# Up-projection of a conv-gated MLP: the Strassen weight sums move from VectorE to accumulating DMAs, and one plain feature tile becomes a Strassen one

## The chip, the core and the metric

The kernel runs on one core of a Trainium2 chip. The metric is device time in microseconds of one launch, as the median of several runs. The engines are called as in the profile: PE is TensorE, DVE is VectorE, ACT is ScalarE, POOL is GpSimd, and SP is SyncE, which here only issues DMAs.

## The reference, cut to what matters

One layer of a decoder: an attention mixer, and after it an MLP. The change is in the first product of the MLP, `h @ w_up`. There are 1024 tokens, a model width of 1024, and 2 x 2816 features (a gate half and a value half); everything is float32.

```python
h = rms_norm(x, pre_ffn_g[l])
u = causal_depthwise_conv(h @ w_up[l], conv_w[l], conv_b[l])   # 3 taps along the tokens
gate, val = jnp.split(u, 2, axis=-1)
y = (jax.nn.gelu(gate, approximate=True) * val) @ w_down[l]
x = x + rms_norm(y, post_ffn_g[l])
```

## The kernel before, in words

**Precision.** Every float32 operand of a product is split in a high part (rounded to the PE's float32r by an ACT copy) and a low part (the rest, by a DVE subtraction): `split`, lines 148 to 151. A product of two such operands takes three matmuls, high by high, low by high, and high by low (`mm3`, lines 153 to 157). So a matmul 128x128 by 128x512 on the page always comes in threes.

**The activations.** After the mixer, `h` lies in SBUF, transposed and split, as `mh` and `ml`, 8 blocks of 128 model rows by 1024 tokens. Line 1363 cuts it in four quarters, b11, b12, b21 and b22 (rows by tokens).

**Plain features.** The 22 feature tiles `f` each hold 128 gate features and 128 value features. A plain feature (`full`, `up`) takes 2 parts x 2 token halves x 8 blocks x 3 = 96 matmuls. The first `FULL` = 3 features are done that way. During them the sums of activations t1 to t4 that Strassen's scheme needs are made: `new_sum` (line 1366) adds and subtracts quarters on DVE and POOL, and the 16 pieces made by `split_sum` (line 1379) split the sums. The raw sums live in the pool `sums`, which holds five tiles of 8 KB a partition: t1, a scratch tile d, t3, t2, t4, in order of first use. The split of t1 is written over b12, so it has to wait until the last plain feature's matmuls have read b12.

**Strassen features.** From `FULL` on, `seven` makes a feature of 7 products (p1 to p7) of 4 blocks x 3 = 84 matmuls. `weights` (line 1412) makes their weight operands for the feature ahead: it loads four raw quarters a11, a12, a21, a22 of 128x512 (SP's queue, `load_raw`, five buffers), makes the four sums s1 = a21 + a22, s2 = s1 - a11, s3 = a11 - a21, s4 = a12 - s2 on DVE (`combined`, line 1423), and splits seven operands (a11, a12, s2, s3, s1, s4, a22). The sums have four buffers with the tag "s" in the pool `mid`; the split operands rotate through 6 + 6 slots in the pools `wpool` and `wb`. The pools `wb` (24 KB a partition) and then `mid` are opened when `sums` is closed, in the same stretch of SBUF, so that, read by sizes, `wb` lies over t1, d and t3, the four "s" buffers lie over the raw t2, and the `u` tiles of `mid` over the raw t4. A buffer can be written only when the last reader of what lay there is done.

**After the products.** `plus` in `seven` adds the products from PSUM (six banks take turns) into the tiles `u` (two buffers each in `uf` for odd features and `mid` for even ones), whose first two columns POOL clears (line 1304). `gated` (line 1336) does the convolution, two DVE instructions for each part (lines 1343 and 1344), the gelu on ACT, the product on DVE (line 1347), and stores the tile `c` on SP's queue.

**Order.** The order on each engine is fixed at build time by a planner that goes by priorities (program order, with `high_priority` moving a piece of work forward) and by its own estimates of durations. Each engine then runs its list in order, and a DMA is issued in its place in the list of the engine that issues it; a wait in the list holds up what stands behind it. For the first Strassen feature, products p1, p2 and p4 are issued first (`early`, line 1497), and its weights are made at a raised priority (line 1490).

Of the kernel before, what the change touches and what calls it, by code (L numbers as in the profile page):

```python
# [18 lines left out]
AF = mybir.ActivationFunctionType  # L19
ALU = mybir.AluOpType  # L20
AX = mybir.AxisListType
PSUM = bass.MemoryType.PSUM
DRAM = bass.MemoryType.DRAM
# [17 lines left out]
C3 = 2 * math.pi - C1 - C2  # L41
NEG = -1.0e30

FULL = 3


NH = NF // 2
# [40 lines left out]
def trunk(ctx: ExitStack, tc: tile.TileContext, a, out):  # L88
    nc = tc.nc
    dma = nc.sync.dma_start  # L90
# [22 lines left out]
    def slot_w(pool=None, bufs=6):  # L113

        return [(pool or wpool).tile([P, 512], F32R, tag=t, name=n, bufs=bufs) for t, n in (("wh", "whi"), ("wl", "wlo"))]

    def load_raw(src, tag="raw", width=512, parts=1):
        raw = (raws_in[-1].tile([P, 512], F32, tag=tag, name="raw") if isinstance(tag, str) else tag)[:, :width]
        if src is None:
            return raw  # L120
        if parts > 1:
            for c in range(0, width, width // parts):
                dma(raw[:, c : c + width // parts], src[:, c : c + width // parts])
            return raw
        to = raw if src.dtype == F32 else raw.bitcast(I32)
        dma(to if len(src.shape) == 2 else to.rearrange("p (b c) -> p b c", c=src.shape[-1]), src)
        return raw
# [20 lines left out]
    def split(hi, lo, src, eng=None):  # L148
        copy = nc.scalar.activation(hi, src, AF.Copy)  # L149
        sub(eng or nc.vector, lo, src, hi)  # L150
        return copy.ins

    def mm3(o, sh, sl, mh, ml, first, last, on=False):

        nc.tensor.matmul(o, sh, mh, start=first, stop=False, skip_group_check=on)  # L155
        nc.tensor.matmul(o, sl, mh, start=False, stop=False, skip_group_check=on)  # L156
        nc.tensor.matmul(o, sh, ml, start=False, stop=last, skip_group_check=on)  # L157
# [42 lines left out]
    def halves():  # L200
        return [slice(i * 512, (i + 1) * 512) for i in range(2)]
# [243 lines left out]
    with ExitStack() as st_y:  # L445
# [166 lines left out]
        made, fetched, again = 12, 14, []  # L612
# [3 lines left out]
        for n in range(8, len(steps_v)):  # L616
# [25 lines left out]
            if k == 0 and (p, i) in places_y:  # L642
                q, name, pool = places_y[p, i]
# [302 lines left out]
    for n in range(2):  # L946
        t = mask_2.rearrange("p (k r) -> p r k", r=2)[:, n]
# [267 lines left out]
    def any_psum():  # L1215
        return next(psums)()

    with st2:
# [50 lines left out]
        for m in range(8):  # L1269
# [22 lines left out]
            s2 = tiny.tile([P, 1], F32, tag="ss1", name="ss2")  # L1292
# [8 lines left out]
        def new_u(pool=uf):  # L1301

            u = pool.tile([P, 2 + S + 30], F32, tag="u", name="u", bufs=2)
            nc.gpsimd.memset(u[:, 0:2], 0.0)
            return u[:, : 2 + S]
# [46 lines left out]
    def full(f):  # L1352

        us = []
        for part in range(2):
            for uu in first_ups[part] if f == 0 else up(f, part):
                for _ in range(min(len(pieces), 3)):
                    pieces.pop(0)()
            us.append(uu)
        gated(f, us)  # L1360
# [18 lines left out]
    def split_sum(name, to=None):  # L1379

        to = to or [xw.tile([P, 4, 512], F32R, tag=name + p, name=name + p) for p in "hl"]
        pieces.extend(functools.partial(split, *(t[:, k] for t in to), raw_sums[name][:, k]) for k in range(4))
        return to
# [3 lines left out]
    with ExitStack() as st_s:  # L1387
# [7 lines left out]
        t3, t2, t4 = (split_sum(n) for n in ("t3", "t2", "t4"))  # L1395
        for f in range(2, FULL):
            full(f)

        first_ws = {}
        for i, name in enumerate(("a11", "a12")):  # L1400
            raw = raw_of_a[name] = load_raw(a["w_up"][2 * FULL][:, halves()[i]])
            first_ws[name] = slot_w()
# [9 lines left out]
    def weights(f, ws=(), a1=()):  # L1412

        a11, a12 = a1 or (load_raw(a["w_up"][2 * f][:, sl]) for sl in halves())
        a21, a22 = (load_raw(a["w_up"][2 * f + 1][:, sl]) for sl in halves())
        ws = dict(ws)

        def put(name, src):
            if name not in ws:
                ws[name] = slot_w(wb if len(ws) % 2 else None)  # L1420
                split(*ws[name], src)

        def combined(name, x, y, op):
            t = mid.tile([P, 512], F32, tag="s", name=name, bufs=4)
            nc.vector.tensor_tensor(t, x, y, op=op)
            return t

        put("a11", a11)
        put("a12", a12)
        if f == FULL:  # L1430
            put("a22", a22)
        s1 = combined("s1", a21, a22, ALU.add)
        s2 = combined("s2", s1, a11, ALU.subtract)
        put("s2", s2)
        put("s3", combined("s3", a11, a21, ALU.subtract))
        put("s1", s1)
        put("s4", combined("s4", a12, s2, ALU.subtract))
        put("a22", a22)
        return ws

    def seven(f, ws, early=()):

        us = [new_u(uf if f % 2 else mid) for _ in range(2)]
        c11, c12, c21, c22 = (u[:, 2 + h * 512 : 2 + (h + 1) * 512] for u in us for h in range(2))
        ops = dict(p1=("a11", b11), p6=("s2", t2), p2=("a12", b21), p7=("s3", t3), p5=("s1", t1), p4=("a22", t4), p3=("s4", b22))
        got = {}

        def made(p):
            if p not in got:
                w, x = ops[p]  # L1450
                got[p] = any_psum()
                for k in range(4):
                    c = slice(k * P, (k + 1) * P)
                    mm3(got[p], ws[w][0][:, c], ws[w][1][:, c], x[0][:, k], x[1][:, k], k == 0, k == 3)
            return got[p]

        def plus(to, p, x):
            nc.vector.tensor_tensor(to, made(p), x, op=ALU.add)  # L1458

        for p in early:  # L1460
            made(p)
        nc.scalar.activation(c11, made("p1"), AF.Copy)
        plus(c22, "p6", c11)
        plus(c11, "p2", c11)
        plus(c21, "p7", c22)
        plus(c12, "p5", c22)
        plus(c22, "p5", c21)
        plus(c21, "p4", c21)
        plus(c12, "p3", c12)
        return us  # L1470


# [9 lines left out]
    def put(step, *srcs):  # L1482

        operands[step] = []
        for src in srcs:
            operands[step].append(next(places)())
            split(*operands[step][-1], src)

    places = iter([lambda: slot_w(early, 2), slot_w] * 2 + [slot_w] * 4)
    with tc.high_priority(offset=40):  # L1490
        ws = weights(FULL, first_ws, raw_of_a.values())
    for f in range(FULL, NF):
        if f + 1 == NF:
            for i in range(AHEAD):
                put(i, load_raw(g_at(0, 0, i)), load_raw(w_at(0, 0, i)))
        following = weights(f + 1) if f + 1 < NF else None
        gated(f, seven(f, ws, ("p1", "p2", "p4") if f == FULL else ()))
        ws = following
# [137 lines left out]
    for n, (p, f) in enumerate(steps):  # L1636
# [9 lines left out]
        if last and f == NH - 3:  # L1646
            prepared = reach(prepared, 6 * NH, prepare)
            st_bv.close()
            more = open_pool(ctx, "more")
# [10 lines left out]
        if p == "p2" and f == 0:  # L1660
            st_az.close()
            norms = open_pool(ctx, "norms", side="right")
            s4 = norms.tile([P, 2, 4], F32, name="s4")
# [6 lines left out]
        if p == "p2" and 2 <= f < 6:  # L1670
# [3 lines left out]
            c22 = ys[4 + m][:, 512:]  # L1674
# [7 lines left out]
    for m in range(4):  # L1682
# [5 lines left out]
        c21 = ys[4 + m][:, :512]  # L1688
# [58 lines left out]
```

## Time and profile before

| | |
|---|---|
| median of 3 runs | 1698.27 us (1698.05 to 1699.11) |
| span of the profiled execution, first to last instruction | 1697.2 us |
| busy PE, DVE, ACT, POOL | 99%, 79%, 52%, 6% |
| granted PE clock, mean over the span | 0.999 |
| plain features on PE | about 1048 to 1116 us |
| Strassen features on PE | about 1116 to 1478 us |

The page gives the profiled execution's span and no separate time of it; what lies around the span is the difference to the runs, 0.9 to 1.9 us. In a timeline row, the columns are start, duration, engine, line, operation, operands by tile name, count, and idle time before it with what ended it.

### The profile page before, as it was taken

The numbers are of one execution on the slowest core, as the hardware profiler recorded it, in microseconds if no ns is written. First come the engines' busy times: TensorE is split into PE (matmuls) and PEld (weight loads), VectorE is DVE, ScalarE is ACT, GpSimd is POOL, SyncE is SP. The second block draws the span as 40 slices with busy tenths as digits, with TensorE's granted clock in tenths as the row PEclk, the third lists the DMA queues.
The fourth block names the chain that finished last, engine by engine and source line by source line (L and its number), as shares of the span: only waits on it lengthen the run. The fifth ranks groups of instructions, "written<-read, shape, count | busy, mean of one in ns | idle before, by whom it ended". The sixth has DMA issues, their size and how long they took to land.

```text
span 1697.2 us, 23030 instructions
## 1 busy us (share of the span) xinstructions
PE 1683.2 (99%) x8076; PEld 1410.1 (83%) x8076; DVE 1344.4 (79%) x2557; ACT 888.9 (52%) x1631; POOL 110.0 (6%) x174
## 2 busy tenths in 40 slices
PE   9999999999999999999999999999999999999997
PEld 7888888888888888888888888888888888888886
DVE  8795686877777776678756865899999989799967
ACT  7643575655544776667653533464344444355453
POOL 0031000000000000000123400300000000000000
PEclk9999999999999999999999999999999999999999
DMA  8767311214112213233675532132222222296524
GB/s 269 231 233 258 99 57 62 88 57 119 50 63 81 69 57 108 82 115 117 208 264 197 198 112 75 38 106 87 99 81 75 93 87 88 84 349 216 194 75 161
DMA packets 104451, 216.41 MB, mean 128 GB/s; under 512 B 12992, under 2 KB 22144, under 8 KB 104336
## 3 DMA queue, kind: packets, MB, share of 16 engines
q1 hardware_dynamic: 89296, 171.28, 30.6%
q0 software_dynamic: 10288, 35.28, 6.2%
q10 hardware_dynamic: 4752, 8.39, 1.3%
q8 instruction: 63, 1.03, 0.3%
q14 instruction: 52, 0.43, 0.1%
HBM read 167.05 MB, written 47.86 MB: 127 GB/s over the span
## 4 chain that ended last, share of the span: by engine, by line
PE 94%; DMA 3%; ACT 1%; DVE 1%; issue 1%; POOL 0%; SPq 0%; DVEq 0%; POOLq 0%
PE acc L155 21%; PE acc L157 21%; PE acc L156 21%; PE acc L1583 3%; PE acc L1581 3%; PE acc L1582 3%; PE o L710 2%; PE pt L697 2%; PE acc L1262 2%; PE acc L1260 2%; PE acc L1261 2%; PE o L713 1%; PE s L156 1%; PE s L157 1%; PE s L155 1%; PE s L766 1%
## 5 line engine op out<-in xcount | busy, mean ns | idle before, releaser
L155 PE MATMUL acc<-xh,whi 128*128 128x512 f32 x768 | 304.2, 396 | 0.0
L157 PE MATMUL acc<-xl,whi 128*128 128x512 f32 x768 | 303.8, 396 | 0.0
L156 PE MATMUL acc<-xh,wlo 128*128 128x512 f32 x768 | 303.1, 395 | 0.0
L149 ACT ACTIVATE whi<-raw 128x512 fp32r<-128x512 f32 (+1 forms) x252 | 156.0, 626 | 184.9 <-PE acc L157 98.4
L146 DVE TENSOR_TENSOR wlo<-raw,whi 128x512 fp32r<-128x512 f32 (+1 forms) x252 | 178.0, 713 | 39.4 <-ACT whi L149 36.7
L157 PEld LDWEIGHTS acc<-xl,whi 128*128 128x128 f32 x768 | 144.4, 188 | 27.7
L156 PEld LDWEIGHTS acc<-xh,wlo 128*128 128x128 f32 x768 | 144.4, 188 | 27.6
L155 PEld LDWEIGHTS acc<-xh,whi 128*128 128x128 f32 x768 | 144.5, 188 | 27.5 <-DVE t L685 0.2
L155 PE MATMUL acc<-mh,whi 128*128 128x512 f32 x400 | 155.8, 390 | 0.3 <-ACT mh L149 0.3
L156 PE MATMUL acc<-mh,wlo 128*128 128x512 f32 x400 | 155.6, 389 | 0.0
L157 PE MATMUL acc<-ml,whi 128*128 128x512 f32 x400 | 155.3, 389 | 0.0
L684 ACT ACTIVATE t<-acc 64x512 f32<-64x512 f32 (+1 forms) x160 | 94.7, 592 | 58.6 <-PE acc L157 56.7
L1458 DVE TENSOR_TENSOR u<-acc,u 128x512 f32<-128x512 f32 x133 | 90.8, 687 | 20.8 <-PE acc L157 20.7
L149 ACT ACTIVATE whi<-s 128x512 fp32r<-128x512 f32 x76 | 46.9, 627 | 102.1 <-PE acc L157 86.9
L685 DVE TENSOR_TENSOR t<-acc,cos 128x512 f32<-128x512 f32 x64 | 44.2, 691 | 58.9 <-ACT t L684 58.3
L155 PEld LDWEIGHTS acc<-mh,whi 128*128 128x128 f32 x400 | 75.1, 188 | 16.0 <-ACT mh L149 0.5
L157 PEld LDWEIGHTS acc<-ml,whi 128*128 128x128 f32 x400 | 75.1, 188 | 15.6
L156 PEld LDWEIGHTS acc<-mh,wlo 128*128 128x128 f32 x400 | 75.1, 188 | 15.5
L1582 PE MATMUL acc<-whi,wlo 128*128 128x512 f32 x220 | 77.5, 389 | 0.0
L1581 PE MATMUL acc<-whi 128*128 128x512 f32 x220 | 76.3, 389 | 0.0
L1583 PE MATMUL acc<-wlo,whi 128*128 128x512 f32 x220 | 73.2, 390 | 0.0
L768 DVE CUSTOM_DVE_ANT_0 s<-s,mask_a 128x512 f32<-128x512 f32 (+3 forms) x96 | 52.0, 553 | 23.2 <-PE s L766 14.6
(389 smaller groups left out, 3950.5 us busy)
## 6 DMA issues: line engine op xcount, KB each, us to landing
raw<-in_w_in SPq DMA_DIRECT2D x96, 256.0 KB, 2.9
raw<-in_w_up SPq DMA_DIRECT2D x88, 256.0 KB, 2.8
raw<-in_w_v SPq DMA_DIRECT2D x71, 256.0 KB, 4.6
raw<-c_d SPq DMA_DIRECT2D x48, 256.0 KB, 3.7
c_d<-c SPq DMA_DIRECT2D x22, 512.0 KB, 2.7
raw<-in_w_down SPq DMA_DIRECT2D x37, 256.0 KB, 4.4
v_d<-yv POOLq DMA_DIRECT2D x32, 256.0 KB, 4.8
gt_d<-gate ACTq DMA_DIRECT2D x32, 256.0 KB, 2.2
```

Of the source, the lines that this page charges most:

```text
L146: eng.tensor_tensor(lo, src, hi.bitcast(F32), op=ALU.subtract)
L149: copy = nc.scalar.activation(hi, src, AF.Copy)
L155: nc.tensor.matmul(o, sh, mh, start=first, stop=False, skip_group_check=on)
L156: nc.tensor.matmul(o, sl, mh, start=False, stop=False, skip_group_check=on)
L157: nc.tensor.matmul(o, sh, ml, start=False, stop=last, skip_group_check=on)
L684: nc.scalar.activation(t1[dst], ps[src], AF.Copy)
L685: nc.vector.tensor_tensor(t2, ps, cos[:, sl], op=ALU.mult)
L768: nc.vector.tensor_tensor_reduce(out=s_sb[:, c0:c1], in0=ps, in1=mask, scale=1.0, scalar=-3.0e38, op0=ALU.add, op1=ALU.max, accum_out=mx[: ...
L1458: nc.vector.tensor_tensor(to, made(p), x, op=ALU.add)
L1581: nc.tensor.matmul(banks[m], gh[:, tk], wh, start=f == 0, stop=False)
L1582: nc.tensor.matmul(banks[m], gl[:, tk], wh, start=False, stop=False)
L1583: nc.tensor.matmul(banks[m], gh[:, tk], wl, start=False, stop=f == NH - 1)
```

## The change

`FULL` goes from 3 to 2, so that feature 2 becomes the first Strassen feature. The four weight sums are no longer made on DVE. Where a sum starts from a block in DRAM, SP loads that block into the sum's buffer; where it starts from a raw tile in SBUF, ACT copies the tile there with its sign turned. What is to be added is then added by a DMA on POOL's queue that accumulates into the buffer: a22 from DRAM to s1, a21 from DRAM to -a11 (giving -s3), s1 from SBUF to -a11 (giving s2), and s2 from SBUF to -a12 (giving -s4). So s3 and s4 come out with the other sign, and the two places that add p7 and p3 subtract them. The raw tile a21 is gone.

```diff
-FULL = 3
+FULL = 2
...
         a11, a12 = a1 or (load_raw(a["w_up"][2 * f][:, sl]) for sl in halves())
-        a21, a22 = (load_raw(a["w_up"][2 * f + 1][:, sl]) for sl in halves())
+        d21, d22 = (a["w_up"][2 * f + 1][:, sl] for sl in halves())
+        a22 = load_raw(d22)
...
-        def combined(name, x, y, op):
+        def combined(name, first, *more):
             t = mid.tile([P, 512], F32, tag="s", name=name, bufs=4)
-            nc.vector.tensor_tensor(t, x, y, op=op)
+            if first.space == DRAM:
+                dma(t, first)
+            else:
+                nc.scalar.activation(t, first, AF.Copy, scale=-1.0)
+            for x in more:
+                nc.gpsimd.dma_start(t, x, accum_op=ALU.add)
             return t
...
-        s1 = combined("s1", a21, a22, ALU.add)
-        s2 = combined("s2", s1, a11, ALU.subtract)
+        s1 = combined("s1", d21, d22)
+        minus_s3 = combined("s3", a11, d21)
+        s2 = combined("s2", a11, s1)
+        minus_s4 = combined("s4", a12, s2)
         put("s2", s2)
-        put("s3", combined("s3", a11, a21, ALU.subtract))
+        put("s3", minus_s3)
         put("s1", s1)
-        put("s4", combined("s4", a12, s2, ALU.subtract))
+        put("s4", minus_s4)
...
-        plus(c21, "p7", c22)
+        nc.vector.tensor_tensor(c21, c22, made("p7"), op=ALU.subtract)
...
-        plus(c12, "p3", c12)
+        nc.vector.tensor_tensor(c12, c12, made("p3"), op=ALU.subtract)
```

## The prediction, on record before the result

> **What bounds the kernel now.** I read the page's first part, then PE's waits, then the busy times of each engine in stretches of the stage that is changed, then the timelines of PE and DVE where the plain features end. First the page, and two rows of the table of waits (the second one is the only wait of PE between 1040 and 1490 us):
>
> ```profile
> span 1697.2 us, 23030 instructions
> PE 1683.2 (99%) x8076; PEld 1410.1 (83%) x8076; DVE 1344.4 (79%) x2557; ACT 888.9 (52%) x1631; POOL 110.0 (6%) x174
> ...
> PE pt L578 <- DVE t4l L575: 1.2, 1, 1.2
> PE acc L155 <- ACT mh L149: 0.3, 1, 0.3
> ```
>
> PE is the bound, and in the stage that is changed it waits for nothing but those 0.3 us. So whatever is taken from another engine there gives no time by itself; time comes from fewer matmuls and goes by new waits of PE. The stretches below (columns: length, then busy time and count of PE, PEld, DVE, ACT, POOL, then granted clock, DMA share, GB/s) are the second and third plain feature and a later Strassen feature:
>
> ```profile
> 1070.00:1092.00 22.00, 22.00 (x99) 18.23 (x98) 22.00 (x11) 10.18 (x15) 8.53 (x3) 1.00 0.16 48
> 1092.00:1114.00 22.00, 22.00 (x98) 18.22 (x98) 22.00 (x26) 14.08 (x23) 0.20 (x2) 1.00 0.14 48
> 1231.00:1250.00 19.00, 19.00 (x86) 15.72 (x85) 17.68 (x25) 8.21 (x12) 0.20 (x2) 1.00 0.25 84
> ```
>
> In the plain features DVE is busy without a gap: there the sums t1 to t4 and their splits are made. That work is done in the time of three plain features, and the change leaves it two.
>
> **What it gains.** One product of 12 matmuls, from its first row to the first of the next:
>
> ```profile
> 1472.53 0.39 PE L155 MATMUL acc<-t4h,whi 128*128 128x512 f32 x1
> ...
> 1475.25 0.39 PE L155 MATMUL acc<-mh,whi 128*128 128x512 f32 x1
> ```
>
> That is 2.72 us, 0.2267 us a matmul. A plain feature of 96 costs 21.76 us, a Strassen feature of 84 costs 19.04. One less plain and one more Strassen feature saves 12 matmuls: **-2.72 us**. This is all the gain there can be, since PE waits for nothing that the rest could shorten.
>
> **The rest of a later feature, engine by engine.** Rows: the three groups of DVE sums between 1136 and 1460 us, an ACT copy and a DVE subtraction of a split from the page, the loads and DMAs of POOL's queue by size and median time to landing, the issues of one POOL line with their landing, and POOL's wait ahead of the clearing of `u`.
>
> ```profile
> L1425 DVE TENSOR_TENSOR s<-raw 128x512 f32<-128x512 f32 x34 | 23.5, 692 | 6.2 <-DMA raw<-in_w_up 5.7
> L1425 DVE TENSOR_TENSOR s<-s,raw 128x512 f32<-128x512 f32 x17 | 11.7, 690 | 0.4
> L1425 DVE TENSOR_TENSOR s<-raw,s 128x512 f32<-128x512 f32 x17 | 11.7, 686 | 0.0
> ...
> L149 ACT ACTIVATE whi<-raw 128x512 fp32r<-128x512 f32 (+1 forms) x252 | 156.0, 626 | 184.9 <-PE acc L157 98.4
> L146 DVE TENSOR_TENSOR wlo<-raw,whi 128x512 fp32r<-128x512 f32 (+1 forms) x252 | 178.0, 713 | 39.4 <-ACT whi L149 36.7
> ...
> raw<-in_w_up SPq DMA_DIRECT2D x88, 256.0 KB, 2.8
> v_d<-yv POOLq DMA_DIRECT2D x32, 256.0 KB, 4.8
> mw<-e_d POOLq DMA_DIRECT2D x24, 256.0 KB, 5.1
> ...
> L535 POOL DMA_DIRECT2D v_d<-yv x32: 542/542/4075, 106.6 to 164.6; - x32
> DMA to landing us min/median/max: 2.7/4.8/9.5
> ...
> POOL u L1304 <- DVE c L1344: 261.7, 32, 24.5
> ```
>
> DVE loses 4 x 0.69 = 2.8 us a feature (17.7 to 14.9 of 19.04). ACT gains three sign-turned copies of 0.63 us (8.2 to 10.1). POOL gains four issues of 0.54 us, 2.2 us. SP keeps four loads of 256 KB. The DMA engines get four more transfers of that size, which also read what they add to: a share of 0.25 goes to between 0.5 and 0.75. Turning an addition into a subtraction in `seven` costs nothing, the same DVE instruction. All of it lies beside PE.
>
> The trace shows no accumulating DMA. From POOL's rows of that size its landing is bounded by 2.7 and 9.5 us; I take **4.8**, the median of the transfers nearest in kind (SBUF involved, 256 KB, same queue), since the DMA engines are far from full here. The sums of one feature are then a chain: load of s1 (2.8), a22 on it (4.8), s1 onto s2 (4.8), split of s2 (0.63 + 0.69), s2 onto s4 beside that. Until its "s" buffer is free for the next feature it takes 2.8 + 9.6 + 1.3 = 13.7 us, less than 19.04. As `weights` works a feature ahead, the later features cost **0**; without that cover p6 would come up to 13.7 us after its raw loads.
>
> The Trainium skill (DMA: Bandwidth & Descriptors, section Anatomy of one DMA, SWDGE path) fits 2.0 us plus bytes over 436 GB/s, about 2.6 us for this size, and the rows of this trace, 4.8 and 5.1, stand above it; by the page's figure the sum below would have 4.7 us of waiting in place of 8.1, and 1700.3 us.
>
> **Where the plain features end.** PE rows first, the first p4 and the first p6 in the kernel before:
>
> ```profile
> 1121.52 0.39 PE L155 MATMUL acc<-t4h,whi 128*128 128x512 f32 x1
> ...
> 1124.24 0.39 PE L155 MATMUL acc<-t2h,whi 128*128 128x512 f32 x1
> ```
>
> Ahead of p4 stand p1 and p2, 24 matmuls or 5.44 us, so the third plain feature ends at 1116.08. Without it, PE is there at **1116.08 - 21.76 = 1094.32**, and through with p1 and p2, which need no sum, at 1099.76. DVE's rows (t3's last addition; t4's first; the split of t2; of t3; t4's second; the split of t4, in two rows; the split of t1; the first weight sum):
>
> ```profile
> 1089.13 2.28 DVE L1374 TENSOR_TENSOR t<-t,d 128x2048 f32<-128x2048 f32 x1
> ...
> 1092.53 2.28 DVE L1376 TENSOR_TENSOR t<-mh,t 128x2048 f32<-128x2048 f32 x1
> ...
> 1095.33 2.48 DVE L146 TENSOR_TENSOR t2l<-t,t2h 128x512 fp32r<-128x512 f32 x4
> 1097.74 0.68 DVE L146 TENSOR_TENSOR wlo<-raw,whi 128x512 fp32r<-128x512 f32 x1
> ...
> 1099.54 2.49 DVE L146 TENSOR_TENSOR t3l<-t,t3h 128x512 fp32r<-128x512 f32 x4
> 1101.95 2.28 DVE L1377 TENSOR_TENSOR t<-t,ml 128x2048 f32<-128x2048 f32 x1
> ...
> 1109.48 1.88 DVE L146 TENSOR_TENSOR t4l<-t,t4h 128x512 fp32r<-128x512 f32 x3
> ...
> 1117.81 2.49 DVE L146 TENSOR_TENSOR ml<-t,mh 128x512 fp32r<-128x512 f32 x4
> 1120.22 0.68 DVE L1425 TENSOR_TENSOR s<-raw 128x512 f32<-128x512 f32 x1
> ```
>
> In the kernel before, t4 is split at 1111.36, ten microseconds ahead of p4. With PE 21.76 us earlier that lead is gone. What the change takes off DVE ahead of it is little: after 1095 some three weight splits like the one at 1097.74, 0.6 us apart in the queue, 1.8 us. In the order shown **t4 is ready at about 1109.5**, t1 (2.48 more) at 1112.0. From the other side: if t4's two steps and its split came at once after 1089.13, they would end at 1089.13 + 2.28 + 2.28 + 2.48 = 1096.2, and p4 would not wait. I take the order shown, as the planner put it there by the same priorities.
>
> The weight sums start late too. The "s" buffers lie over the raw t2, whose last reader is its split, ending at 1097.8. From there: s3 (ACT copy 0.63, accumulation 4.8, split 1.3) at 1104.5; s2 (load 2.8, twice 4.8, split 1.3) at 1111.5, but its slot in `wb` lies over t1 and is free at 1112.0, so 1113.3; s4 (4.8 after s2 landed at 1110.2, split 1.3) at 1116.3. Then PE: p7 can start at 1104.5, **4.7 us of waiting**; it ends at 1107.2, p4 starts at 1109.5, **2.3 more**, and ends at 1112.2; p6 at 1113.3, **1.1 more**; p5 and p3 follow without a wait. Sum 8.1 us. Bounds: 0 (landing 2.7 and t4 first) and 20 (landing 9.5: s2 ready at 1120.9, and each product behind its sum). Late next is p6 of the second Strassen feature: its s1 is loaded from 1113 on, s2 ready at 1126.7, PE past p1 of that feature at 1124.1; p2 fills the gap, so I add nothing (bound 2.6). After that 13.7 against 19.04 us gains the lead back.
>
> A wait this long may also slow PE behind it. At the kernel's start the matmuls come 0.43 us apart up to the fourth row here, 0.23 after it:
>
> ```profile
> 8.37 0.63 PE L156 MATMUL s<-whi,xl 128*128 128x512 f32 x1
> 8.80 0.63 PE L157 MATMUL s<-wlo,xh 128*128 128x512 f32 x1
> 9.22 0.63 PE L156 MATMUL pt<-whi,xl 128*128 128x512 f32 x1
> 10.02 0.40 PE L156 MATMUL pt<-whi,xl 128*128 128x512 f32 x1
> 10.25 0.40 PE L157 MATMUL pt<-wlo,xh 128*128 128x512 f32 x1
> ```
>
> Some ten matmuls at 0.2 us more are 2.0 us. Later waits reach only 1.2 us and slow nothing, so the cost lies between 0 and 2.0; I take 0 and keep the other end as a rival.
>
> **Sum.** The profiled span 1697.2 lies 1.07 us under the median of the runs, and nothing around it changes: 1698.27 - 2.72 + 8.1 = **1703.7 us**.
>
> **The rivals.** *Hidden (not slower).* The planner gives DVE and the sums another order when PE would stand still: t4 first, convolutions of the plain features later, the split of t2 two microseconds earlier. For it: p4 can be ready at 1096.2 by the rows; PE has p1, p2, p4, p7, p5, 13.6 us, ahead of p6. Against it: DVE is full from 1070 on, and p6 at 1111.5 is still later than 1094.32 + 13.6 = 1107.9. With landings under 3 us, or a chain that starts 4 us sooner, PE waits nothing: 1695.5. It decides as soon as t2 is split before 1094 and t4 before 1102.
>
> *Slow pace after the wait.* PE resumes at 0.43 us a matmul for a while: 1703.7 + 2.0 = 1705.7. For it: the start of the kernel. Against: no row after the start. The Trainium skill (TensorE: Matmul & The Clock Gate, Part 1, What's actually happening) has such a rule, half the clock after an idle window of about 3.4 us until a busy one has passed; the first wait here, 4.7 us, is over it, and by its figure some 1.7 us would be lost; the start of this trace agrees with the half pace, and no wait of that length stands in the trace.
>
> *The chain of accumulations becomes the bound.* It decides from a landing of (19.04 - 2.8 - 1.3) / 2 = 7.5 us on. At 8.5 us a feature takes 21.1 us, 2.06 us more in each of 19: 1703.7 + 39 = 1743. For it: landings up to 9.5 us; and on POOL the DMAs queue behind the clearing of `u`, which waits 8.2 us on average (261.7 over 32) for DVE to release the tile; 13.7 + 8.2 is over 19.04 too, 2.9 us a feature, 55 us in all. Whoever waits for these DMAs then are ACT and DVE with the splits, and the additions out of PSUM behind them. Against it: those waits are of a queue with nothing else to do, the median landing would have to grow by half, and the DMA engines are a quarter busy.
>
> *It doesn't do what it says.* The 2.8 us of DVE a feature are not on the path at all; that part is worth 0 in the sum already.
>
> **Chances.** What can be told from no change is about 0.2%, 3.4 us, so 1694.9 to 1701.7. Waiting as forecast 0.38 (0.09 of it short enough to end under 1701.7), slow pace 0.14, hidden 0.30 (0.03 of it under 1694.9), the chain 0.14, others 0.04 (half of them gains). Faster 0.05, same 0.27 + 0.09 + 0.02 = 0.38, slower 0.57. The range: 1694.8 takes in the hidden case; 1714 leaves out most of the chain's 0.14 and little else. The forecast's own: 1699 to 1709.
>
> **What would show it.** PE waits of several microseconds in the table, for ACT or DVE on t4, or on s sums, all between 1095 and 1125, and none later; the first p4 row about 10 us after the end of p2; POOL DMAs landing in about 5 us; DVE near 15 us of 19 in later features; Strassen features 19.04 us apart. Wrong it would be if PE's row shows no wait there (hidden), if waits recur in every feature (the chain), or if one of the features past the third is longer than 19.1 us.

## The result, and the profile after

The kernel after takes 1722.85 us (median of 4 runs, 1719.33 to 1724.08), the kernel before in the same comparison 1698.69 us: a ratio of 1.0141, 95% interval 1.0129 to 1.0153. The change costs 24.2 us. 1703.7 us was forecast, within 1694.8 to 1714.0: slower was right, but the loss is 4.5 times the 5.4 us that were forecast.

The page's first part for the kernel after, then PE's waits between 1050 and 1520 us (us in total, times, longest):

```profile
span 1721.8 us, 23296 instructions
PE 1688.9 (98%) x8064; PEld 1409.8 (82%) x8064; DVE 1305.7 (76%) x2491; ACT 919.4 (53%) x1691; POOL 175.9 (10%) x254
```

```profile
PE acc L155 <- ACT whi L149: 7.8, 2, 6.0
PE acc L155 <- ACT t4h L149: 4.4, 1, 4.4
PE acc L157 <- DVE t4l L146: 3.5, 1, 3.5
PE acc L155 <- DVE u L1466: 1.9, 2, 1.4
PE acc L155 <- ACT u L1470: 0.6, 1, 0.6
PE acc L155 <- ACT mh L149: 0.3, 1, 0.3
```

The 12 matmuls are gone (8064 for 8076), and DVE is 39 us less busy. In exchange PE, which waited 0.3 us in this stage, now waits for t4, for two splits of weight sums (`whi`), and for banks of PSUM (`u`, the tile into which the bank's reader adds or copies).

In PE's timeline the first of these waits stand here (the last column is the idle time and what ended it); four rows behind the longest of them follow its first row:

```profile
1103.51 0.80 PE L155 MATMUL acc<-t4h,whi 128*128 128x512 f32 x1 [4.42 <-ACT t4h L149]
1108.19 0.80 PE L157 MATMUL acc<-t4l,whi 128*128 128x512 f32 x1 [3.46 <-DVE t4l L146]
1119.08 0.79 PE L155 MATMUL acc<-t3h,whi 128*128 128x512 f32 x1 [6.00 <-ACT whi L149]
...
1120.40 0.63 PE L157 MATMUL acc<-t3l,whi 128*128 128x512 f32 x1
1120.83 0.63 PE L155 MATMUL acc<-t3h,whi 128*128 128x512 f32 x1
...
1122.92 0.40 PE L157 MATMUL acc<-t3l,whi 128*128 128x512 f32 x1
1123.16 0.39 PE L155 MATMUL acc<-t3h,whi 128*128 128x512 f32 x1
...
1125.78 0.49 PE L155 MATMUL acc<-t2h,whi 128*128 128x512 f32 x1 [1.78 <-ACT whi L149]
```

To compare kernels I add up, over PE's rows from 1060 to 1520 us, the time from one matmul's start to the next beyond 0.227 us; waits and slow matmuls both go into it. This *lost time* is 0.6 us before and 27.8 after: 17.9 between 1100 and 1120 us, 5.5 between 1120 and 1140, 3.9 between 1160 and 1200, nothing later. 27.2 more lost, less 2.7 of matmuls, is 24.5 us: the measured 24.2, within the scatter of the runs.

The busy times of that stretch and of a later feature, columns as in the prediction:

```profile
1093.00:1115.00 22.00, 12.05 (x39) 8.18 (x37) 21.84 (x26) 12.17 (x20) 2.26 (x7) 0.77 0.20 59
1115.00:1131.00 16.00, 10.11 (x27) 7.29 (x28) 3.96 (x7) 5.12 (x9) 3.57 (x5) 0.68 0.79 161
1300.00:1319.00 19.00, 19.00 (x86) 15.73 (x85) 14.85 (x20) 9.77 (x15) 3.64 (x6) 1.00 0.60 139
```

First DVE is full while PE does 39 matmuls in 22 us; then DVE and ACT work 4.0 and 5.1 of 16 us, PE does 27 matmuls, and the DMA engines are busy (0.79): the splits wait for the accumulations, and PE for the splits. A later feature looks as forecast: DVE 14.9, ACT 9.8, DMA share 0.60, PE without a gap.

Why the accumulations are late, in the timelines of ACT and of POOL:

```profile
1107.63 1.24 ACT L1342 ACTIVATE c<-u,cw 128x1024 f32<-128x1024 f32 x1 [2.61 <-DVE c L1347]
1109.37 1.06 ACT L1346 ACTIVATE c<-c 128x1024 f32<-128x1024 f32 x1 [0.50 <-DVE c L1344]
1111.23 0.60 ACT L1470 ACTIVATE u<-acc 128x512 f32<-128x512 f32 x1 [0.81 <-DVE t4l L146]
1111.73 1.66 ACT L1429 ACTIVATE s<-raw 128x512 f32<-128x512 f32 x3
1118.40 0.63 ACT L149 ACTIVATE whi<-s 128x512 fp32r<-128x512 f32 x1 [5.01 <-DMA s<-in_w_up]
1125.10 1.15 ACT L149 ACTIVATE whi<-s 128x512 fp32r<-128x512 f32 x2 [6.07 <-DMA s<-s]
```

```profile
1111.20 0.17 POOL L1304 MEMSET u<- 128x2 f32 x2 [1.62 <-DVE t4l L146]
1112.78 1.78 POOL L1431 DMA_DIRECT2D s<-in_w_up  x2 [1.42 <-ACT s L1429]
...
1121.81 0.86 POOL L1431 DMA_DIRECT2D s<-s  x1 [7.14 <-issue]
```

The sign-turned copies stand in ACT's list behind the gelu of a plain feature and behind the copy of p1 out of PSUM, and that copy waits for t4's split, since its `u` tile lies over the raw t4. So the chain of weight sums, which needs nothing of t4, starts when t4 is done, at 1111.7. Its first two accumulations are slow as well, 5.6 and 7.7 us from issue to landing against a median of 4.0.

### The profile page after: what moved, and what is told of

It reads as the page before. It is cut to its first block, busy times and chain, and to the rows that moved or that the text cites. A ratio compares the mean times of both kernels' runs of the same rounds, so it can differ in the third digit from the quotient of the medians.

```text
span 1721.8 us, 23296 instructions
## 1 busy us (share of the span) xinstructions
PE 1688.9 (98%) x8064; PEld 1409.8 (82%) x8064; DVE 1305.7 (76%) x2491; ACT 919.4 (53%) x1691; POOL 175.9 (10%) x254
## 5 line engine op out<-in xcount | busy, mean ns | idle before, releaser
L155 PE MATMUL acc<-mh,whi 128*128 128x512 f32 x384 | 150.5, 392 | 1.6 <-ACT u L1470 0.6
L156 PE MATMUL acc<-mh,wlo 128*128 128x512 f32 x384 | 149.4, 389 | 0.0
L157 PE MATMUL acc<-ml,whi 128*128 128x512 f32 x384 | 149.1, 389 | 0.0
L1466 DVE TENSOR_TENSOR u<-acc,u 128x512 f32<-128x512 f32 x100 | 68.8, 688 | 28.9 <-PE acc L157 28.5
L146 DVE TENSOR_TENSOR wlo<-s,whi 128x512 fp32r<-128x512 f32 x80 | 55.0, 689 | 30.9 <-ACT whi L149 30.9
```

The source lines that it names most:

```text
L146: eng.tensor_tensor(lo, src, hi.bitcast(F32), op=ALU.subtract)
```

## The experiments

A number behind "lost" is the lost time as defined above, taken from the one profiled execution of a run; the runs of one kernel scatter by 1 to 6 us. Medians of the kernel before in these comparisons were 1698.2 to 1699.0 us.

**The two parts of the change apart.** First the accumulating DMAs with three plain features:

```diff
-FULL = 2
+FULL = 3
```

> The changed kernel with three plain features again (FULL = 3), so only the accumulating DMAs are new against the kernel before. Theory (the loss sits where the plain features end, because two of them are too short for the sums): PE comes 21.8 us later to sums that are made at the same time, so it waits 0 to 5 us there and nothing later: 1698 to 1704 us. Rival (the DMA sums cost time in every feature): most of the loss stays, 1715 us or more.

Then the kernel before with two:

```diff
-FULL = 3
+FULL = 2
```

> The kernel before with FULL = 2, the weight sums still on DVE. Theory: 2.7 us fewer matmuls, and a wait for the split of t4 as in the changed kernel (about 8 us), then weight sums on DVE behind it (2 to 4 us) and up to 2 us of slow matmuls: 1704 to 1711 us. Rival (the DMA sums are the cause, and two plain features suffice): 1695 to 1699 us.

Measured: 1709.08 us (1.0063, 1.0048 to 1.0078), lost 10.8; and 1712.96 us (1.0086, 1.0069 to 1.0103), lost 17.8. Their waits of PE, first three plain features with DMA sums, then two with DVE sums:

```profile
PE acc L155 <- ACT whi L149: 3.2, 2, 2.6
PE acc L155 <- DVE u L1466: 2.4, 2, 1.6
...
PE acc L155 <- ACT u L1470: 0.8, 1, 0.8
```

```profile
PE acc L155 <- ACT t4h L149: 4.4, 1, 4.4
PE acc L157 <- DVE t4l L146: 3.5, 1, 3.5
PE acc L155 <- ACT whi L149: 3.1, 2, 2.9
```

The first came out between the forecasts of its theory and its rival, the second above its theory's range. The costs, 10.4 and 14.2 us, add up to 24.6, near the change's 24.2. So there are two causes: t4 is late because a plain feature is missing, whoever makes the weight sums; and the chain of DMAs costs ten microseconds even where t4 is in time.

**The first feature's sums on DVE again, later ones by DMA.**

```diff
+        if f == FULL:
+            s1 = on_dve("s1", a21, a22, ALU.add)
+            s2 = on_dve("s2", s1, a11, ALU.subtract)
+            minus_s3 = on_dve("s3", a21, a11, ALU.subtract)
+            minus_s4 = on_dve("s4", s2, a12, ALU.subtract)
+        else:
+            s1 = combined("s1", d21, d22)
...
```

> The changed kernel, but the four weight sums of the first Strassen feature alone are made on DVE from four raw tiles; all later ones by accumulating DMAs. Theory: the waits of 6.0 and 1.8 us for the first DMA sums go, the wait for t4 (7.9 us) stays: 1706 to 1713 us. Rival (the later features lose the time): 1717 us or more.

1721.26 us (1.0130, 1.0115 to 1.0145), lost 26.0: the rival's range, not the theory's. The waits for the first feature's splits shrink (2.7 us for `whi` in place of 7.8), yet a new one stands around 1165 us:

```profile
PE acc L155 <- DVE u L1478: 5.5, 1, 5.5
```

PE waits for a bank of PSUM, whose reader is an addition on DVE. In DVE's list that addition stands behind a weight split that waits 7.3 us for ACT's half of it, and so for a DMA sum. The lag of the chain doesn't go away with the first feature; it goes to the second.

**PE's clock.** 36 matmuls into an unused bank ahead of p4 and 28 ahead of p7 keep PE busy while it would wait (nothing reads their results):

```diff
         for p in early:
+            if p == "p4":
+                filler(36)
             made(p)
+        if early:
+            filler(28)
+            made("p7")
```

> The changed kernel with 64 matmuls into an unused PSUM bank where PE waits, 36 ahead of p4 and 28 ahead of p7 of the first Strassen feature, so that PE does not stand still there; they compute nothing that is used, and everything that is needed is still computed. Theory: the arrival of p4, p7 and p6 is set by the sums, so the slow matmuls behind the first two waits cost nothing and only those behind the last one do: 1 to 3 us faster than the changed kernel, 1720 to 1722 us. Rival A (each slow stretch counts, some 29 matmuls at 0.2 us): 5 to 6 us faster, 1717 us. Rival B (slow matmuls cost nothing): the same as the changed kernel, 1722.9 us, or slower by filler that comes too late.

1722.1 us (1.0136, 1.0121 to 1.0151): not to be told from the change. The granted clock between 1093 and 1131 us rises to 0.91; in the kernel after it is 0.73. The filler takes 64 x 0.227 = 14.5 us, and 10.9 are still lost: 25.4 in all, against 27.8. The slow matmuls are real, but a gain of 5 to 6 us from fast ones (rival A) is excluded: PE still waits for t4 behind the first filler (0.5 us) and for a split of a sum behind the second (1.8 us). A gain of 1 to 3 us, the theory, can't be told from none.

**SP's queue.** The load of a21 for the first s1 (1108.02) follows a store of `c` (1107.56) on SP. This run has the two plain features' stores on ACT's queue:

```diff
-        dma(c_d[f], cs[0])
+        (nc.scalar.dma_start if f < FULL else dma)(c_d[f], cs[0])
```

> The changed kernel with the stores of the two plain features' tiles c issued from ACT's queue, so that the load of s1 doesn't stand behind a store on SP's queue that waits for DVE (it was issued at 1108.0 us); the lists of PE, DVE and POOL are unchanged. Theory A (the first DMA sums are late because their sign-turned copies stand in ACT's list behind work that waits for the split of t4, at 1111.7): the load comes some 10 us earlier and nothing else moves, 1721 to 1724 us. Rival B (SP's queue holds the sums up): the waits ahead of p7 and p6 shrink, 1714 to 1719 us.

The load now goes out at 1096.59, right behind the end of t2's split (1096.5), so its buffer was free by then. 1721.62 us (1.0140, 1.0125 to 1.0155), and the wait for s3's split is still 6.6 us: ACT's copies go out at 1111.2 and POOL's first accumulation at 1112.3, as late as before. The store isn't the cause.

**An early start of the chain.** The first feature's four sums go to buffers of the pool `early` that nothing else uses at that time:

```diff
-            t = mid.tile([P, 512], F32, tag="s", name=name, bufs=4)
+            if f == FULL:
+                t = early.tile([P, 512], F32, tag=next(spare), name=name, bufs=2)
+            else:
+                t = mid.tile([P, 512], F32, tag="s", name=name, bufs=4)
```

> The changed kernel with the first Strassen feature's four sums in buffers that lie free during the plain features (those kept for the next product), so that they need not wait for the raw t2 to be read; made by the same DMAs. Theory (the late start of the chain of sums costs the waits ahead of p7 and p6, and its lag the 4 us of the next features): s sums are there before t4, the wait for t4 (8.4 us) and some slow matmuls stay, 1706 to 1713 us. Rival (the chain is too slow in any feature): 1716 us or more.

The same with three plain features:

> The same early buffers with three plain features. Theory: with the first sums made in time and t1 to t4 split in time nothing is left to wait for, 1698 to 1701 us, like the kernel before. Rival (accumulating DMAs hold up ACT and DVE in every feature, whatever the start): 1704 to 1709 us as with three plain features and the late start.

1710.11 us (1.0073, 1.0057 to 1.0090), lost 12.2, of it 10.0 around the waits for t4 (5.0 and 1.8 us); and 1701.41 us (1.0020, 1.0011 to 1.0029), lost 4.1, just above its theory's range. In the first the copies on ACT now start at 1060.9 and the accumulations at 1072.5, long before t4. One buffer choice takes 12.7 us off the change (12.2, when each is taken against the runs of the kernel before in its own comparison), and 7.7 off the version with three plain features, in which this row alone is left of the waits for the chain:

```profile
PE acc L155 <- ACT whi L149: 1.9, 1, 1.9
```

So of the ten microseconds of the DMA sums, three stay and the rest was the late start.

**Other products first, and DVE's order by hand.** With the early buffers, p3, which needs no t sum, in place of p4 among the first products:

```diff
-        gated(f, seven(f, ws, ("p1", "p2", "p4") if f == FULL else ()))
+        gated(f, seven(f, ws, ("p1", "p2", "p3") if f == FULL else ()))
```

> Early buffers, two plain features, and the first Strassen feature begins with p1, p2, p3 in place of p1, p2, p4: p3 needs no sum of activations, only s4. Theory: 12 more matmuls (2.7 us) stand ahead of the first product that waits for t4, t2 or t3, so 2 to 4 us less than the early buffers alone, 1703 to 1710 us. Rival (s4 is made last in the chain, so p3 waits in t4's place): no gain against the early buffers alone.

1708.10 us (1.0055, 1.0040 to 1.0070), lost 11.6, within the theory's range; but now PE waits 5.2 us for s4's split, which stands on DVE behind t1's: the rival's wait, though not its time.

Then t4's two steps and its split were put ahead of everything on DVE by ordering edges (`issue_after`, behind the last split's DVE instruction, `lows[0]`), and s3, s4 and the plain features' convolutions behind all of it, with the accumulating DMAs and with DVE sums; PE takes p1, p2, p4, p6 and p5 first. In both of these runs the difference on POOL that goes into t3 reads the quarter b12 after t1's split has been written over it, and the first plain feature's convolutions read `u` tiles that hold the second's values; instructions and sizes are the same, so the time stands for the work, with t3 late.

The core of the edit:

```diff
+        def in_turn(fn=None):
+            with tc.high_priority(offset=80), tc.issue_after(lows[0]):
...
+        in_turn(puts["a22"])
+        t2 = split_sum("t2")
+        in_turn()
+        in_turn(puts["s2"])
+        t1 = split_sum("t1", b12)
+        in_turn()
+        in_turn(puts["s1"])
+        in_turn(lambda: new_sum("t3", b22, b12, nc.gpsimd))
```

> The changed kernel, with the first Strassen feature's four sums in free buffers, and with DVE's order around the end of the plain features fixed by hand: the two additions of t4 right behind t2's, then the splits of t4, a22, t2, s2, t1, s1, the last addition of t3, the splits of t3, s3, s4, and only then the convolutions of both plain features. Theory (it is the order on DVE and the late start of the sums, not the amount of DVE work, that makes PE wait): t2's second addition ends at 1086.6 in the changed kernel; from there 2.2 + 2.2 + 2.4 us and two weight splits bring t4 at about 1094.6, t2 1097.6, t1 1100.6, t3 1106, s4 1107. PE comes to p4 at 1098.9 and needs p7 at 1107.1, so it waits under 1 us there, and with some 1.7 us lost later, as with early buffers alone, the time is about 1698.5 us. Rival (the sums t1 to t4 are too much work for two plain features in any order): PE still waits 6 us or more, and the time is 1704 us or more.

> The kernel before with two plain features, all weight sums on DVE, the first feature's sums in free buffers and the same order by hand. Theory: PE waits under 1 us at the end of the plain features, and nothing is lost in later features, since no chain of DMAs is there; the 12 matmuls less are then seen at last: 1698.5 - 2.7 + 0.5 = about 1696.3 us, the first version that is not slower than the kernel before. Rival (too much DVE work): the four sums come on top of it, PE waits 6 us or more, 1702 us or more.

1714.18 us (1.0092, 1.0075 to 1.0109) and 1716.33 us (1.0101, 1.0086 to 1.0116): the theory missed, and the time is in the rival's range. t4 is in time, but p4 waits for a bank, 11.1 us and 10.7 us, and what ends the wait is ACT's copy of p1, which stands behind work for the late t3. The run with DMA sums shows one thing more, on DVE and POOL:

```profile
1090.73 5.11 POOL L1374 TENSOR_TENSOR t<-mh 128x2048 f32<-128x2048 f32 x1 [11.50 <-ACT mh L151]
1095.80 4.99 POOL L1375 TENSOR_TENSOR d<-ml 128x2048 f32<-128x2048 f32 x1
```

```profile
1091.29 5.10 DVE L148 TENSOR_TENSOR wlo<-s,whi 128x512 fp32r<-128x512 f32 x1
1096.31 5.03 DVE L148 TENSOR_TENSOR wlo<-raw,whi 128x512 fp32r<-128x512 f32 x1
```

A split of 0.68 us takes 5 us on DVE: it ends some 0.6 us after the POOL subtraction beside it, as if it had begun only then.

The same by hand with POOL's part and the first feature's convolutions left where they were, and p3 ahead of p7; the diff is against the two runs above:

```diff
+        add_t3 = new_sum("t3", b22, b12, nc.gpsimd, hold=True)
...
+        in_turn(puts["s4"])
-        in_turn(lambda: new_sum("t3", b22, b12, nc.gpsimd))
+        in_turn(add_t3)
```

> The changed kernel, with the first Strassen feature's four sums in free buffers, t3's two subtractions on POOL where they were, the first plain feature's convolutions where they were, and DVE's order behind them fixed by hand: t4's additions and split, then the splits of a22, t2, s2, t1, s1, s4, then t3's last addition and its split, s3, and then the second plain feature's convolutions; PE takes p1, p2, p4, p6, p5, p3, p7. Theory (the order on DVE and the late start of the sums, not the amount of DVE work, make PE wait): with t2's second addition ending at 1086.6, as in the changed kernel, and three convolutions (3.6 us) ahead, t4 is split at about 1097, t2 at 1100, t1 at 1103, t3 at 1109; PE needs p4 at 1098.9 and p7 at 1109.8 and waits under 2 us in all. With some 1.7 us lost later, as with early buffers alone, the time is about 1699 us. Rival (too much DVE work for two plain features in any order): PE waits 6 us or more and the time is 1704 us or more.

> The kernel before with two plain features, all weight sums on DVE, the first feature's sums in free buffers and the same order by hand. Theory: the four sums put 2.8 us more on DVE ahead of t4, so that PE waits 1 to 3 us at the end of the plain features, and nothing is lost in later features, where no chain of DMAs is: 1698.3 - 2.7 + 2 = about 1697.5 us. Rival (too much DVE work): 6 us of waiting or more, 1702 us or more.

1706.92 us (1.0054, 1.0040 to 1.0068) and 1706.78 us (1.0049, 1.0037 to 1.0062), lost 11.4 each. The rival's times came (1704 or more, and 1702 or more), but its reason, too much work on DVE for two plain features, is not borne out by the last pair of runs below. Nothing waits for t4's split any more in the first (0.6 us in the second); in its place come waits for banks again (5.1 us in the first, for ACT's copies of p1 of this feature and later ones; 5.0 us in the second).

**POOL beside DVE.** The kernel before has the same thing in its first plain features; its rows on POOL and DVE:

```profile
1062.11 6.75 POOL L1372 TENSOR_TENSOR t<-mh 128x2048 f32<-128x2048 f32 x1 [97.62 <-ACT mh L149]
1068.82 4.60 POOL L1373 TENSOR_TENSOR d<-ml 128x2048 f32<-128x2048 f32 x1
1076.25 5.01 POOL L1373 TENSOR_TENSOR d<-ml 128x2048 f32<-128x2048 f32 x1 [2.83 <-DVE t L1374]
```

```profile
1062.11 2.28 DVE L1372 TENSOR_TENSOR t<-mh 128x2048 f32<-128x2048 f32 x1
...
1069.80 4.17 DVE L146 TENSOR_TENSOR wlo<-raw,whi 128x512 fp32r<-128x512 f32 x1 [4.80 <-ACT whi L149]
1076.70 6.71 DVE L1376 TENSOR_TENSOR t<-mh,t 128x2048 f32<-128x2048 f32 x1
```

The subtraction of 6.71 us is of the form that takes 2.28 in the prediction's row at 1092.53. In both cases POOL had begun first. Where both begin at 1062.11, DVE has its 2.28 us, and POOL is the one that takes longer, 6.75 in place of some 4.6 to 5.0. The next runs have the three subtractions of t1 and t3 on DVE, early buffers and p3 first, with DVE sums and with DMA sums:

```diff
-            (eng or nc.vector).tensor_tensor(t, f(x[0]), f(ys[0]), op=ALU.subtract)
-            nc.gpsimd.tensor_tensor(d, f(x[1]), f(ys[1]), op=ALU.subtract)
+            nc.vector.tensor_tensor(t, f(x[0]), f(ys[0]), op=ALU.subtract)
+            nc.vector.tensor_tensor(d, f(x[1]), f(ys[1]), op=ALU.subtract)
```

> The kernel before with two plain features, weight sums on DVE (the first feature's in free buffers), p3 in place of p4 among the products issued first, and the three subtractions of t1 and t3 that POOL did moved to DVE. Theory (DVE stands still while POOL's 128x2048 subtractions run: some 4.8 + 3.5 + 4.4 = 12.7 us of waiting and stretched instructions between 1064 and 1084): three times 2.28 us of DVE work replace it, t3 is split about 6 us earlier, t4 at about 1106, and PE, which has p1, p2, p3 and p7 till 1109.8 with p7 no longer late, waits 3 us or less: 1698.2 - 2.7 + 3 = about 1698.5 us. Rival (DVE's own work is the limit): 6.8 us more of it, PE waits 10 us or more, 1705 us or more.

> The same with the accumulating DMAs of the change in place of the DVE sums (against early buffers with p3 alone, 1708.1 us, only the three subtractions move). Theory: 2.8 us less of DVE work ahead of t4, PE waits 2 us or less at the end of the plain features, and the 1.7 us that the chain of DMAs cost later with early buffers stay: about 1699.5 us. Rival: no change against 1708.1 us, or slower by some 5 us.

1706.58 us (1.0043, 1.0030 to 1.0057), lost 10.4; and 1704.78 us (1.0035, 1.0022 to 1.0047), lost 8.3. That subtraction is back at its length, in the run with DVE sums:

```profile
1076.01 2.28 DVE L1376 TENSOR_TENSOR t<-mh,t 128x2048 f32<-128x2048 f32 x1
```

With DMA sums t4's split ends at 1106.9, against 1111.7 with p3 first alone, though DVE has 6.8 us more to do, and the time falls by 3.3 us. So the standing still was part of it. But both runs were forecast to wait 3 us or less and lose more; the first came out in the rival's range (1705 or more), though its longest wait, 6.0 us, is not for t4 but for the split of s2: its slot in `wb` lies over t1, and in ACT's and DVE's lists it stands behind t4's split, in both runs.

**Slots.** s4, s3 and s2 get slots over nothing, s1 and a22 those over t1; they are split in that order, a22 last, and PE's order is p1, p2, p3, p7, p6, p5, p4. So the edit moves three things at once; its line on the slots:

```diff
-                ws[name] = slot_w(wb if len(ws) % 2 else None)
+                ws[name] = slot_w(wb if (name in ("s1", "a22") if f == FULL else len(ws) % 2) else None)
```

> The run with accumulating DMAs, early buffers and the subtractions on DVE (1704.8 us), with the first feature's split operands s4, s3 and s2 in slots over nothing, s1 and a22 in those over t1, and PE's order p1, p2, p3, p7, p6, p5, p4. Theory (only the places in the lists matter): t4 at 1106.9 is needed at 1109.8; s1's split, about 1108.6, lets p5 wait 1.5 us from 1107.1 on; with 1.2 us lost later, the 2.7 us of matmuls are paid back in full: 1698.5 - 2.7 + 1.5 + 1.2 + 0.5 = about 1699 us. Rival (some 7 us stay at this place in another form): 1704 us or more.

> The same with the weight sums on DVE. Theory: 1 to 3 us of waiting at the end of the plain features and none later: 1698.5 - 2.7 + 2 = about 1698 us. Rival: 1704 us or more.

With DMA sums 1708.48 us (1.0061, 1.0048 to 1.0074), lost 11.9, only 2.0 of it between 1100 and 1120: slower than the run before it, since the Strassen features behind the first lose 9.3 (waits of 2.6 us for the split of the next s2 and 2.5 for a bank, and shorter ones); why they lose more than there wasn't tested. With DVE sums 1703.09 us (1.0029, 1.0018 to 1.0041), lost 7.3, nearly all of it for s1. Both theories, about 1699 and 1698 us, missed.

Last, all five in slots over nothing, and p1 copied out of PSUM to a free buffer, at a raised priority:

```diff
+                ws[name] = slot_w(wb if f > FULL and len(ws) % 2 else None)
...
-        nc.scalar.activation(c11, made("p1"), AF.Copy)
+        base = early.tile([P, 512], F32, tag="wl", name="base", bufs=2) if f == FULL else c11
+        with tc.high_priority(offset=60 if f == FULL else 0):
+            nc.scalar.activation(base, made("p1"), AF.Copy)
```

> Two plain features, DVE sums, t1 and t3 wholly on DVE, PE's order p1, p2, p3, p7, p6, p5, p4 as in the run of 1703.1 us, with the split operands of the first Strassen feature in slots over nothing and p1 copied to a free buffer. Theory (only places in the lists matter): the 5.4 us of waiting for s1 become 0 to 2 us, since s1 is split ahead of t4 and t4, about 1111, is needed at 1109.9: about 1698 to 1700 us, no slower than the kernel before for the first time. Rival: the wait moves to another place with the same size, 1703 us or more.

> The same with the accumulating DMAs of the change (against 1708.5 us). Theory: the 2 us at the end of the plain features go, while the 9 us that the second to fourth Strassen feature lost (waits of 2.8 us for the split of its second sum and 2.6 us for a bank) stay, since they come from the chain of DMAs: about 1705 to 1707 us. Rival (these losses follow from the first): under 1702 us.

With DVE sums 1698.78 us (1.0003, 0.9994 to 1.0012), lost 3.1: as fast as the kernel before, with two plain features, as its theory had it. With DMA sums 1702.99 us (1.0026, 1.0016 to 1.0037), below its theory's range and above its rival's, lost 6.1, 5.6 of it behind 1120. PE's waits of this stage, beside the 0.3 us at its beginning that all versions have, with DVE sums and then with DMA sums:

```profile
PE acc L155 <- DVE u L1465: 1.7, 1, 1.7
```

```profile
PE acc L155 <- ACT whi L149: 3.1, 1, 3.1
...
PE acc L155 <- ACT u L1477: 1.8, 1, 1.8
```

So two plain features are enough for t1 to t4, even with more work on DVE than in the change: the order, the slots and POOL's part made the difference, though these runs don't price each alone. 2.5 us are still lost more than before, which is what the 12 matmuls give. The accumulating DMAs then cost 4.2 us (1702.99 - 1698.78). No version was faster than the kernel before.

## Why the prediction was wrong

The step that failed is the start of the chain of weight sums: the forecast counted it from the moment its buffers are free, and it waited some 14 us longer in the lists of the engines that issue it.

- **The start of the chain is the term that was mis-sized most.** The forecast of s3 at 1104.5, s2 at 1113.3 and s4 at 1116.3 counts from the moment the buffers are free, 1097.8. They were free (in the run with the stores on ACT's queue the load goes into one at 1096.6), but the issuing engines were not: SP's load came at 1108.0, ACT's copies at 1111.7, POOL's first accumulation at 1112.8. The length from there was about right for s3 (5.4 forecast from its copy to its split, 6.7 measured, 1111.7 to 1118.4) and short for s2, whose first accumulation (a22 onto s1) landed after 7.7 us in place of 4.8. So p7 started 14.6 us late (1119.1) and p6 12.5 (1125.8). That the queues hold up what stands behind a wait was said of POOL's clearing of `u` in a rival and not applied to this step. The run with early buffers shows it: 12.7 us less by the buffers alone.
- **PE's order** failed too, in the step "p7 can start at 1104.5, 4.7 us of waiting; it ends at 1107.2, p4 starts at 1109.5". PE's list is fixed, and p4 stands in it right behind p2, as the description of the kernel says of `early`. p4 could not give way to p7; its first matmul had to wait for ACT's t4h (4.4 us) and its third for DVE's t4l (3.5 us), 7.9 us where 2.3 were forecast for t4. This moved waiting from p7 to p4 more than it added: p4 ends at about 1113.1, forecast 1112.2.
- **t4 at 1109.5** was near, its split ends at 1111.1, but partly by luck: DVE's order was not the one shown. The three weight splits ahead of it are gone, 1.8 us, and all rows of this stage come 0.8 us earlier, as PE's do; but t1's split, which the prediction put behind t4's, stands ahead of it:

```profile
1103.92 2.48 DVE L146 TENSOR_TENSOR ml<-t,mh 128x512 fp32r<-128x512 f32 x4
...
1109.26 1.88 DVE L146 TENSOR_TENSOR t4l<-t,t4h 128x512 fp32r<-128x512 f32 x3
```

- **The gain, 2.72 us, was right**: lost time and this gain together give the measured difference, after and in the run with DVE sums and free slots (3.1 - 0.6 - 2.7 = -0.2 us by the trace, 0.5 us by the medians).
- **PE's arrival** was right: forecast 1094.32 and 1099.76, measured 1093.49 and 1098.93.
- **Later features at 0** failed for the next few: 3.9 us after 1160 in the kernel after, 4.2 in the run with three plain features, 5.5 in one wait where only the first feature's sums were made by DVE. "p2 fills the gap, so I add nothing (bound 2.6)" saw only the split that is late, not what is queued behind it: the additions that empty PSUM. Behind 1200 us the 0 held, as the 13.7 us chain against 19.04 said.
- **The prices.** The landing was taken at 4.8 and has a median of 4.0 us, but the first two, on which p7 and p6 hang, took 5.6 and 7.7. POOL's issue was taken at 0.54 and is 0.85 (4 of them 3.4 us a feature, beside PE). With a landing of 2.6 us the forecast would not have come down to 4.7 us of waiting, nor to none with landings under 3 us: by its own rows p4 waits for t4 until 1109.5 and p6 for s2's split, in the slot over t1, until 1113.3 all the same, and the sum stays 8.1.
- **The chain as the bound** did not come (steady features as forecast, PE without a gap), though its mechanism, ACT and DVE waiting with the splits and the additions behind them, is what cost those 3.9 us for a while. **Hidden** did not come either: the planner moved t1's split ahead of t4's and not t4 forward, and it took early buffers, free slots and another order on PE, by hand, to get there.
- **The slow pace** came as the rival described, longer: some 25 matmuls between 1093 and 1131, most of them 0.43 us apart, lose 5.8 us. The Trainium skill (TensorE: Matmul & The Clock Gate, Part 1, What's actually happening) has half the clock after an idle window of some 3.4 us, and the trace agrees: after 6.0 us of waiting the slow rows run from 1119.1 to 1122.9. (The wait of 1.2 us that the prediction names as the longest later one is at 1.25 us, at the kernel's start; the later ones reach 0.84 us.) But a price of its own it is not shown to be: with filler the clock was up, and the time lay within the scatter of the change's runs.
- **"DVE is busy without a gap"** read stretched rows as work: 3.5 and 4.4 us between 1069.8 and 1083.3 are standing still beside POOL.

What stays open: how much of the loss at the end of the plain features falls to DVE's order and how much to ACT's, since each run that moved one uncovered the other; whether the 4.2 us of the DMA sums would go with other priorities for these features; and why the first two accumulations landed so late.

## What to carry to other kernels

The time at which a buffer is free or an operand ready is only a lower bound for the start of a chain: for each first instruction look in its engine's list for what stands ahead of it and what that waits for, on every engine the chain passes (here SP, ACT, POOL, and DVE for the split), and PE's own list too. Here, work moved from one engine to a chain over three gained nothing, since PE is the bound, and it paid for each of those lists at the start. Where a lead of ten microseconds (t4 before) is about to be used up, price what comes behind it at its place in the lists and not at its length.

## What the runs showed of the hardware

The accumulating DMAs of 256 KB, by the page's two rows and by the answer for POOL's line:

```profile
s<-in_w_up POOLq DMA_DIRECT2D x40, 256.0 KB, 4.0
s<-s POOLq DMA_DIRECT2D x40, 256.0 KB, 3.9
```

```profile
DMA to landing us min/median/max: 3.2/4.0/7.7
```

The source, DRAM or SBUF, makes no difference to the median; the slowest, 7.7 us, is one of the first two, which were issued 0.6 us apart. Each issue holds POOL 0.85 us, against 0.54 for the plain ones of the kernel before. All these landings stand above the 2.6 us that one estimates for this size by the fit of the Trainium skill (DMA: Bandwidth & Descriptors, Anatomy of one DMA, SWDGE path); the measurement decides.

A DVE instruction with two inputs in SBUF that comes to a POOL subtraction of 128x2048 already running stands still until that ends, and the profile counts it as busy: 5.10 for 0.68, 6.71 for 2.28 us. Where both began at once, POOL was the one held up: 6.75 us, 2.15 more than the next one's 4.60, beside a DVE subtraction of 2.28. The Trainium skill (Trainium Architecture — The Big Picture, What this means for kernel authors) calls the port pair that DVE and GpSimd share "an exclusive lock (not a bandwidth split)"; the rows agree.
